# When the job of the token sums is spawned: ahead of attention's output product instead of behind it

## The chip, the cores and the metric

The kernel runs on one core of a Trainium2 chip. The metric is the device time of one execution in microseconds (us), as the median of several runs. The engines of the core are named as the profile names them: PE is the matrix engine (PEld its weight loads), DVE the vector engine, ACT the scalar engine, POOL and SP the other two; SP here only issues transfers (DMA). Each engine takes its instructions in the order in which the program lists them.

## The reference

Two layers act on x of 256 tokens by 2048 columns. Layer 0 mixes tokens by forgetting attention, layer 1 by dilated attention; behind each stands an MLP with a hidden width of 8192. Everything is float32. What matters here, cut down:

```python
def sq_relu_mlp(h, w_up, w_down):
    a = jax.nn.relu(h @ w_up)
    return (a * a) @ w_down

for i in range(DEPTH):
    h = rms_norm(x, mix_norm_g[i])
    mix = fox_attention(h, ...) if i % 2 == 0 else dilated_attention(h, ...)
    x = x + mix                       # the last step of attention is o @ w_out
    h = rms_norm(x, mlp_norm_g[i])
    x = x + sq_relu_mlp(h, mlp_w_up[i], mlp_w_down[i])
```

## The kernel before, in words

**Products.** A float32 product is made of three matmuls: each operand is split into a rounded high half and the low rest, and high x high, high x low and low x high are added in PSUM. The tokens are the stationary side (two blocks of 128), the weights the moving side (512 columns at a time). Weights arrive in *pieces* of 256 rows by 512 columns, in tiles `raw`, five of which exist. For each piece ACT writes the high half `wh` (L398, a cast), then DVE writes the low half `wl` (L399, a subtraction): together *the split* of the piece. Five tiles of each half exist too. A piece is 12 matmuls in an ordinary product (L447 to L449), 6 in a *slot* (below; L1114 to L1116). SP issues the loads of `raw` (L373); a tile is loaded again when its split is through.

**The program's order is made by ticks.** `product_steps` issues the matmuls of one step of 128 rows and then calls `jobs.tick()`; so an ordinary piece is two ticks and a slot one. When a piece's matmuls are issued, the split of the piece five further on is issued, just ahead of the tick that ends it. All other work is written as generators, *jobs*. A job yields a number (sleep so many ticks) or a key (sleep until another job has entered the key in `done`). `Jobs._run` goes once through the list of living jobs, oldest spawn first, and lets each that is due issue its instructions; it is called at each tick and at each spawn from outside. A key that a younger job enters is therefore seen by an older one at the next call only. `pin` fixes the order in which the instructions were issued, engine by engine. `clear(steps)` adds one tick where needed to end on a chosen parity of the tick count; slots flip that parity through `shift`.

**Around the change.** `out_proj` (attention's output product) makes four chunks of 512 columns of x: the first three interleaved (`group=3`), the fourth by itself, eight pieces. Behind each chunk `add_chain` adds it to x on DVE (L975) and spawns `norm_chain`, which sleeps 2 ticks, transposes the chunk on DVE and writes it to DRAM by SP (L531, L354), 3 ticks later has SP read it back, and after 11 more ticks (9 for the first chunk) splits it into `hT` (ACT L549, DVE L550), the stationary side of the MLP, two keys `(tag, pr)` a chunk, one tick apart. There are eight keys, `pr` 0 to 7. Later ACT takes sums of squares (`junk_n`, L614).

**The MLP** (`mlp`) opens with two chunks interleaved (pieces 0 to 15, counted from the MLP's start), the first 12 steps of the one, 12 of the other, and then the last 4 of each. Among the ordinary pieces that follow stand *slots*: some chunks of the up product are done with 7 products in place of 8 (Strassen-Winograd on 2x2 blocks), from sums of weight blocks (`sd`, `v`: L395, L401, L402 on DVE, ahead of or between the splits that use them) and from sums of token blocks. Up chunks that are through go by `up_chain` and `turn_up`: ACT takes relu and square (L1009, L1013, two each), DVE transposes (L1032), a round trip through DRAM follows, then ACT and DVE split again (L1057; L1061 and L1064).

**`token_sums(tag)`** makes the sums of token blocks, for both MLPs ("n1", "n3"), one *set* for each of the eight keys: four adds on DVE into one tile `room` (L563, L566, L567, L568), two ticks later a cast on ACT (L582), one tick later a subtraction on DVE (L586) that gives the low half; the last set has two of either. Each set first waits for its key and for `clear(4)` ticks. The first use of a set is a slot behind piece 15 (`jobs.need(("sums", tag, pr))`). The job issues no transfers. In the kernel before it is spawned by `mlp`, at L1143, when `out_proj` has issued everything.

Of the kernel before, what the change touches and what calls it, by code (L numbers as in the profile page):

```python
# [9 lines left out]
F32 = mybir.dt.float32  # L10
# [7 lines left out]
P = 128  # L18
# [101 lines left out]
def trunk(ctx: ExitStack, tc, x, fox_w_in, fox_b_f, fox_q_gain, fox_k_gain, fox_w_out, dil_w_in,  # L120
          dil_q_gain, dil_k_gain, dil_w_out, mix_norm_g, mlp_norm_g, mlp_w_up, mlp_w_down, out):
    nc = tc.nc
    jobs = Jobs()
# [4 lines left out]
    def clear(steps):  # L128

        return steps + (jobs.now + steps + 1 + shift[0]) % 2  # L130
# [21 lines left out]
    work = ctx.enter_context(tc.tile_pool(name="work", bufs=1))  # L152
# [317 lines left out]
    def in_group(new, steps, posts, parts=PARTS):  # L470


        banks = []
        for a, b in parts:
            for n, post in enumerate(posts):
                if a == 0:
                    banks.append(new(n))
                steps(banks[n], range(a, b))
                if b == KC:
                    jobs.spawn(post(banks[n]))  # L480
# [74 lines left out]
    def token_sums(tag):  # L555


        to = work.tile([P, 4, P], F32, tag="vw", name=f"room_{tag}", bufs=1)
        for pr in range(KC // 2):
            yield (tag, pr)  # L560
            yield clear(4)
            whole = hT[tag][pr]
            nc.vector.tensor_add(to.rearrange("p (i t) n -> p i (t n)", i=2), whole[:, :, 0, :].bitcast(F32),  # L563
                                 whole[:, :, 1, :].bitcast(F32))
            a12, a22, a11, a21 = (to[:, i, :] for i in range(4))
            nc.vector.tensor_add(a21, a21, a22)  # L566
            nc.vector.tensor_sub(a11, a11, a21)  # L567
            nc.vector.tensor_add(to[:, 0:2, :], to[:, 0:2, :], a11.unsqueeze(1).to_broadcast([P, 2, P]))  # L568
            yield 2
            if pr < KC // 2 - 1:  # L570
                split_sums = [[work.tile([P, 4, P], F32R, tag=SUM_TAGS[2 * pr + x], name=f"sums_{tag}_{pr}_{x}", bufs=1)
                               for x in range(2)]]
            else:
                three = [work.tile([P, 3, P], F32R, tag="s", name=f"sums_{tag}_{pr}_{x}", bufs=S_BUFS) for x in range(3)]
                split_sums = [three[0:2], (three[2][:, 0:1, :], three[2][:, 1:2, :])]
            sumT[tag, pr] = tuple([x[:, i, :] for x, _ in parts for i in range(x.shape[1])] for parts in
                                  (split_sums, [pieces[::-1] for pieces in split_sums]))
            at = 0
            spans = []
            for hi, lo in split_sums:  # L580
                spans.append(to[:, at:at + hi.shape[1], :])
                nc.scalar.copy(hi, spans[-1])  # L582
                at += hi.shape[1]
            yield 1
            for (hi, lo), of in zip(split_sums, spans):
                nc.vector.tensor_sub(lo, of, hi.bitcast(F32))  # L586
            jobs.done.add(("sums", tag, pr))
# [166 lines left out]
    def heads_pairs(name, slot):  # L754


        whole = work.tile([P, 2, 2, P], F32, tag=f"qkw{slot}", name=f"{name}w", bufs=1)
        q = work.tile([P, 2, 2, P], F32R, tag=f"q{slot}", name=f"{name}q", bufs=1)
        k = [work.tile([P, 2, S], F32R, tag=f"k{x}{slot + 3}", name=f"{name}k{x}", bufs=1) for x in "hl"]
        return (whole[:, 0], q[:, 0], q[:, 1]), (whole[:, 1], *k)  # L760

    def values(name):
        whole = work.tile([P, NC], F32, tag="vw", name=f"{name}w", bufs=1)
        both = work.tile([P, 2, NC], F32R, tag="v", name=f"{name}hl", bufs=1)
        return whole, both[:, 0], both[:, 1]
# [171 lines left out]
    def dilated(tag):  # L937
        for q4 in range(4):
            qTs, kTs = zip(*(heads_pairs(f"d{q4}_{g}", g) for g in range(3)))
            vt = values(f"dv{q4}")  # L940

            def heads_post(g):
                return lambda acc: qk_chain(acc, tag, ("dqk", q4, g),
                                            [(0, 2, DIL_G + g, qTs[g]), (2 * P, 2, DIL_G + 3 + g, kTs[g])])

            def value_post(acc):
                return v_chain(acc, tag, ("dv", q4), vt)

            if q4 == 0:
                in_group(lambda n: sums(), lambda acc, ks: product_steps(acc, keys_h(tag), lhs_h(tag), ks),  # L950
                         [value_post, heads_post(0)])
            for g in range(1 if q4 == 0 else 0, 3):
                product(keys_h(tag), lhs_h(tag), heads_post(g))
            for i in range(2):
                jobs.spawn(dil_head(q4, i, qTs, kTs, vt))
            if q4:
                product(keys_h(tag), lhs_h(tag), value_post)
# [33 lines left out]
    def out_proj(keys, lhs, then=None, ready=None, scale=None, group=0, parts=OUT_PARTS, late=False):  # L991
        posts = [lambda acc, n=n: add_chain(acc, n, then, ready, scale, late) for n in range(NX)]
        if group:
            in_group(lambda n: sums(*(() if n < 2 else (ps_sc, "sc") if scale else (ps_tp, "tp"))),
                     lambda acc, ks: product_steps(acc, keys(0), lhs, ks), posts[0:group], parts)
        for n in range(group, NX):
            if ready is not None and n == NX - 1:
                last_product(keys(n), lhs, final_add(n, scale))
            else:
                product(keys(n), lhs, posts[n])  # L1000
# [122 lines left out]
    def mlp(tag, **after):  # L1123
        aTs = [{} for b in range(4)]
        banks = []

        def one(b, n, what, pr):
            if pr == 0 and what in (0, 2):
                pools = ((ps_acc, f"acc{1 - turn['only']}"),) if what else ((ps_tp, "tp"), (ps_sc, "sc"))
                banks[2 * what:] = [pool.tile([P, NC], F32, tag=of, name=f"wide_{tag}_{b}_{n}_{of}{i}")  # L1130
                                    for pool, of in pools for i in range(2)]
            if what < 3:
                jobs.need(("sums", tag, pr))

            def then():
                if what == 2 and pr == KC // 2 - 1:
                    jobs.spawn(wide_chain(list(banks), tag, b, n, aTs[b]))
                if what == 3 and pr == KC // 2 - 2:
                    jobs.reach((f"{tag}a{b}", "crossed", n))

            slot_steps(tag, banks, what, pr, then)

        jobs.spawn(token_sums(tag))  # L1143
        woven.update(count=0, do=one, due={})
        for at, slot in wide_slots():
            woven["due"].setdefault(at, []).append(slot)
        for b in range(4):
            key = f"{tag}a{b}"
            aT = aTs[b]
            posts = [lambda acc, n=n, key=key, aT=aT: up_chain(acc, key, n, aT) for n in range(4)]  # L1150
            if b == 0:
                only = turn["next"]
                in_group(lambda n: sums(), lambda acc, ks: product_steps(acc, keys_h(tag), lhs_h(tag), ks), posts[0:2])
                turn["only"] = only
            for n in UP_ALONE[b]:
                product(keys_h(tag), lhs_h(tag), posts[n])

            def chunks(n):
                def at(k):
                    if n == NX - 1:  # L1160

                        jobs.done.add((tag, "free", b, k // 4 - 1))
                    return key, k // 4
                return at

            if b == 3:
                turn.update(next=turn["only"], only=None)
            out_proj(chunks,
                     lambda k: (aT[k // 4][0][:, k % 4, :], aT[k // 4][1][:, k % 4, :]),
                     scale=tag, group=3 if b == 3 else 0, parts=LAST_DOWN_PARTS, **(after if b == 3 else {"late": True}))  # L1170
            jobs.done.add((tag, "free", b, NX - 1))
        woven["do"] = None
# [66 lines left out]
    tag = "n0"  # L1239
    for j in range(4):  # L1240
# [10 lines left out]
        for hh in range(4):  # L1251
            jobs.spawn(fox_head(j, hh, qT, kT, vt))
        product(keys_h(tag), lhs_h(tag), lambda acc: v_chain(acc, tag, ("fv", j), vt))

    out_proj(lambda n: lambda k: ("of", k),
             lambda k: (oT["f", k // 4][0][:, k % 4, :], oT["f", k // 4][1][:, k % 4, :]),
             normed("n1", MLP_G), group=3)
    jobs.spawn(dilation_tables())
    mlp("n1", then=normed("n2", KC))
    dilated("n2")  # L1260
    out_proj(lambda n: lambda k: ("od", k // 2),
             lambda k: (oT["d", k // 4][0][:, k % 4, :], oT["d", k // 4][1][:, k % 4, :]),
             normed("n3", MLP_G + KC), group=3)
# [32 lines left out]
```

## Time and profile before

| what | value |
|---|---|
| median of 3 runs | 2091.22 us (2090.2 to 2091.6) |
| time of the profiled execution | 2090.77 us |
| its span from the first instruction to the last | 2089.0 us |
| PE, PEld busy | 2078.6 us, 1817.7 us |
| DVE, ACT, POOL busy | 1730.0 us, 1294.6 us, 275.2 us |
| granted clock of PE | 1.000 |

The page gives shares over the whole span; the stretches that matter lie at the two MLP beginnings, at 365 us ("n1") and at 1443 us ("n3"). A timeline row has the start, the time (for several instructions merged: from the first start to the last end), the engine, the line, out<-in, a count, and in brackets how long the engine was idle before and for whom. The time from one row's start to the next is what an instruction costs in a busy queue; it is a little shorter than its own duration, since neighbours overlap. A windows row has for a stretch each engine's busy time, then the granted clock and the transfers.

### The profile page before, as it was taken

The page shows a single profiled execution, that of the slowest core. Times are in us where ns is not written, and L with a number is a line of the kernel's source. Part 1 is how long each engine was busy: PE and PEld are TensorE (multiplying, and loading weights), DVE is VectorE, ACT ScalarE, POOL GpSimd, SP SyncE. Part 2 cuts the span into 40 slices and gives each one's busy share as a digit, 9 for nine tenths or more (in the row PEclk, how much of TensorE's full clock was granted, in tenths as well). Part 3 has the DMA queues.
Part 4 walks back from the last instruction along what each step waited for, and adds up shares of the span by engine and source line. Part 5 has one row for each costly group of instructions (what it writes and reads, how often), then busy time and mean ns, then how long its engine had stood idle before and what let it go on. Part 6 is the DMA issues. An engine that isn't in the chain of part 4 may idle for free.

```text
span 2089.0 us, 28961 instructions
## 1 busy us (share of the span) xinstructions
PE 2078.6 (100%) x9835; PEld 1817.7 (87%) x9835; DVE 1730.0 (83%) x2215; ACT 1294.6 (62%) x1777; POOL 275.2 (13%) x398
## 2 busy tenths in 40 slices
PE   9999999999999999999999999999999999999999
PEld 7888888878888888888888888888888888888888
DVE  6888876998989889888668787767998898899874
ACT  6665654766666667564656565655666666666662
POOL 2000000111212112120010010000113031212120
PEclk9999999999999999999999999999999999999999
DMA  8888887888888899897877876867879888899885
GB/s 258 255 262 261 257 248 215 272 262 265 269 282 268 264 296 274 262 289 246 278 242 230 248 241 210 268 205 235 269 247 277 281 276 263 276 280 281 263 282 164
DMA packets 357205, 539.04 MB, mean 258 GB/s; under 512 B 43752, under 2 KB 144448, under 8 KB 357056
## 3 DMA queue, kind: packets, MB, share of 16 engines
q1 hardware_dynamic: 334624, 507.41, 76.5%
q0 software_dynamic: 22016, 29.38, 6.2%
q8 instruction: 77, 1.26, 0.2%
q10 hardware_dynamic: 416, 0.39, 0.1%
q14 instruction: 72, 0.59, 0.1%
HBM read 484.09 MB, written 40.39 MB: 251 GB/s over the span
## 4 chain that ended last, share of the span: by engine, by line
PE 89%; DVE 6%; DMA 2%; ACT 1%; issue 1%; SPq 0%; POOL 0%; DVEq 0%; ACTq 0%; POOLq 0%
PE acc L448 23%; PE acc L447 23%; PE acc L449 23%; DVE wl L399 3%; PE wide_n_tp L1115 2%; PE wide_n_tp L1116 2%; PE wide_n_tp L1114 2%; PE wide_n_acc L1116 2%; PE wide_n_acc L1115 2%; PE wide_n_acc L1114 2%; PE wide_n_sc L1115 2%; PE wide_n_sc L1116 1%; PE wide_n_sc L1114 1%; DMA raw<-in_mlp_w_up_dram 1%; ACT wh L398 1%
## 5 line engine op out<-in xcount | busy, mean ns | idle before, releaser
L399 DVE TENSOR_TENSOR wl<-raw,wh 128x1024 fp32r<-128x1024 f32 (+1 forms) x763 | 918.6, 1213 | 303.3 <-ACT wh L398 293.8
L398 ACT CAST wh<-raw 128x1024 fp32r<-128x1024 f32 (+1 forms) x763 | 787.0, 1045 | 503.1 <-PE acc L449 360.8
L448 PE MATMUL acc<-wl,hT_n 128*128 128x512 f32 x1280 | 486.2, 380 | 4.0 <-DVE wl L399 3.8
L447 PE MATMUL acc<-wh,hT_n 128*128 128x512 f32 x1280 | 486.4, 380 | 0.1
L449 PE MATMUL acc<-wh,hT_n 128*128 128x512 f32 x1280 | 485.3, 379 | 0.0
L448 PEld LDWEIGHTS acc<-wl,hT_n 128*128 128x128 f32 x1280 | 242.1, 189 | 40.0 <-DVE wl L399 7.6
L449 PEld LDWEIGHTS acc<-wh,hT_n 128*128 128x128 f32 x1280 | 241.9, 189 | 34.4 <-DVE hT_n L606 0.4
L447 PEld LDWEIGHTS acc<-wh,hT_n 128*128 128x128 f32 x1280 | 242.1, 189 | 33.4 <-ACT hT_n L605 0.7
L447 PE MATMUL acc<-wh,aTh_n1a 128*128 128x512 f32 x512 | 194.0, 379 | 0.0
L448 PE MATMUL acc<-wl,aTh_n1a 128*128 128x512 f32 x512 | 194.0, 379 | 0.0
L449 PE MATMUL acc<-wh,aTl_n1a 128*128 128x512 f32 x512 | 194.0, 379 | 0.0
L447 PE MATMUL acc<-wh,aTh_n3a 128*128 128x512 f32 x480 | 181.9, 379 | 0.0
L448 PE MATMUL acc<-wl,aTh_n3a 128*128 128x512 f32 x480 | 181.9, 379 | 0.0
L449 PE MATMUL acc<-wh,aTl_n3a 128*128 128x512 f32 x480 | 181.9, 379 | 0.0
L970 POOL DMA_DIRECT2D x<-y_n x96 | 84.5, 1326 | 479.2 <-ACT y_n L969 421.0
L398 ACT CAST wh<-sd 128x1024 fp32r<-128x1024 f32 x80 | 84.1, 1051 | 98.1 <-DVE sd L395 75.8
L398 ACT CAST wh<-v 128x1024 fp32r<-128x1024 f32 x80 | 84.1, 1051 | 51.6 <-PE acc L449 41.5
L449 PEld LDWEIGHTS acc<-wh,aTl_n1a 128*128 128x128 f32 x512 | 96.8, 189 | 13.8
L447 PEld LDWEIGHTS acc<-wh,aTh_n1a 128*128 128x128 f32 x512 | 96.8, 189 | 13.7
L448 PEld LDWEIGHTS acc<-wl,aTh_n1a 128*128 128x128 f32 x512 | 96.8, 189 | 13.7
L399 DVE TENSOR_TENSOR wl<-v,wh 128x1024 fp32r<-128x1024 f32 x80 | 97.4, 1217 | 5.7 <-ACT wh L398 4.6
L449 PEld LDWEIGHTS acc<-wh,aTl_n3a 128*128 128x128 f32 x480 | 90.7, 189 | 12.9
(661 smaller groups left out, 3224.1 us busy)
## 6 DMA issues: line engine op xcount, KB each, us to landing
raw<-in_mlp_w_up_dram SPq DMA_DIRECT2D x296, 512.0 KB, 4.9
raw<-in_mlp_w_down_dram SPq DMA_DIRECT2D x256, 512.0 KB, 5.2
raw<-in_dil_w_in_dram SPq DMA_DIRECT2D x192, 256.0 KB, 3.7
raw<-in_fox_w_in_dram SPq DMA_DIRECT2D x94, 512.0 KB, 4.9
raw<-in_fox_w_out_dram SPq DMA_DIRECT2D x32, 512.0 KB, 4.9
raw<-in_dil_w_in_dram SPq DMA_DIRECT2D x32, 512.0 KB, 5.4
raw<-in_dil_w_out_dram SPq DMA_DIRECT2D x32, 512.0 KB, 4.5
x<-y_n POOLq DMA_DIRECT2D x96, 128.0 KB, 6.2
```

The lines of the kernel that those rows point to most:

```text
L398: nc.scalar.copy(hi[:, part, :], raw[:, part, :])
L399: nc.vector.tensor_sub(lo[:, part, :], raw[:, part, :], hi[:, part, :].bitcast(F32))
L447: nc.tensor.matmul(acc[t], ah[:, tok], hi, start=first, stop=False)
L448: nc.tensor.matmul(acc[t], ah[:, tok], lo, start=False, stop=False)
L449: nc.tensor.matmul(acc[t], al[:, tok], hi, start=False, stop=last)
L970: nc.gpsimd.dma_start(xt[n][:, t, h * HC:h * HC + HC], y, accum_op=ALU.add)
L1114: nc.tensor.matmul(banks[bank], ah, wh, start=what < 3 and of == 0, stop=False, **alone)
L1115: nc.tensor.matmul(banks[bank], ah, wl, start=False, stop=False, **alone)
L1116: nc.tensor.matmul(banks[bank], al, wh, start=False, stop=of == KC // 2 - 1, **alone)
```

## The change

The spawn of `token_sums` moves out of `mlp` to the place in `trunk` ahead of `out_proj`, for both MLPs. The generator then starts before its first key exists, so the tile `room` is allocated when the first key is there.

```diff
     def token_sums(tag):
 
 
-        to = work.tile([P, 4, P], F32, tag="vw", name=f"room_{tag}", bufs=1)
         for pr in range(KC // 2):
             yield (tag, pr)
+            if pr == 0:
+                to = work.tile([P, 4, P], F32, tag="vw", name=f"room_{tag}", bufs=1)
             yield clear(4)
...
-        jobs.spawn(token_sums(tag))
         woven.update(count=0, do=one, due={})
...
+    jobs.spawn(token_sums("n1"))
     out_proj(lambda n: lambda k: ("of", k),
...
     jobs.spawn(dilation_tables())
     mlp("n1", then=normed("n2", KC))
     dilated("n2")
+    jobs.spawn(token_sums("n3"))
     out_proj(lambda n: lambda k: ("od", k // 2),
```

## The prediction

> **What bounds the kernel now.** I read the page, then PE's waits, then the windows of the two MLP beginnings, then the timelines of DVE, ACT and SP there.
>
> ```profile
> span 2089.0 us, 28961 instructions
> PE 2078.6 (100%) x9835; PEld 1817.7 (87%) x9835; DVE 1730.0 (83%) x2215; ACT 1294.6 (62%) x1777; POOL 275.2 (13%) x398
> ```
>
> PE bounds it: matmuls follow one another without a gap.
>
> ```profile
> 365.03 0.38 PE L449 MATMUL acc<-wh,oTfl 128*128 128x512 f32 x1
> 365.25 0.38 PE L447 MATMUL acc<-wh,hT_n 128*128 128x512 f32 x1
> ...
> 456.22 0.48 PE L448 MATMUL acc<-wl,hT_n 128*128 128x512 f32 x1 [1.29 <-DVE wl L399]
> ```
>
> One matmul is 0.216 us, so a piece of 12 is 2.59 us, and "n1" starts at 365.25. Nothing gives PE less to do. A time can change only by PE waiting more or less, so I look for its waits.
>
> ```profile
> core 0: us, PE busy (x) PEld busy (x) DVE busy (x) ACT busy (x) POOL busy (x), PEclk, DMA share, GB/s
> 365.25:406.69 41.44, 41.44 (x194) 36.29 (x192) 37.27 (x69) 32.57 (x64) 1.07 (x1) 1.00 0.86 284
> 406.69:460.00 53.31, 50.82 (x230) 42.58 (x229) 51.45 (x70) 32.60 (x43) 13.20 (x24) 1.00 0.79 251
> 1484.80:1538.10 53.30, 50.87 (x230) 42.66 (x229) 51.44 (x70) 32.63 (x43) 13.05 (x24) 1.00 0.79 253
> ```
>
> From 406.69 to 460.00 run pieces 16 to 40: 13 ordinary pieces and 12 slots, 228 matmuls, 49.25 us at 0.216. They take 53.31, so PE loses 4.06 us, the last and largest loss at piece 39 (the row at 456.22, waiting for `wl`); "n3" loses the same. DVE is busy for 51.45 of the 53.31: here the splits are late because DVE has too much in front of them. These 8.1 us are all that could be won. The price of the sums, in DVE's and ACT's queues:
>
> ```profile
> 374.47 1.13 DVE L550 SCALAR_TENSOR_TENSOR hT_n<-turned_n,gain,hT_n 128x128 fp32r<-128x128 f32 x4
> 375.52 1.22 DVE L399 TENSOR_TENSOR wl<-raw,wh 128x1024 fp32r<-128x1024 f32 x1
> ...
> 377.70 1.30 DVE L531 STREAM_TRANSPOSE turned_n<-x 128x512 f32<-128x512 f32 x2
> 378.93 1.18 DVE L399 TENSOR_TENSOR wl<-raw,wh 128x1024 fp32r<-128x1024 f32 x1
> 380.03 0.68 DVE L563 TENSOR_TENSOR room_n<-hT_n 128x512 f32<-128x512 f32 x1
> ...
> 381.40 0.43 DVE L568 TENSOR_TENSOR room_n<-room_n 128x256 f32<-128x256 f32 x1
> 381.74 1.22 DVE L399 TENSOR_TENSOR wl<-raw,wh 128x1024 fp32r<-128x1024 f32 x1
> 383.46 1.23 DVE L399 TENSOR_TENSOR wl<-raw,wh 128x1024 fp32r<-128x1024 f32 x1 [0.50 <-ACT wh L398]
> 384.60 0.69 DVE L586 TENSOR_TENSOR sums_n<-room_n,sums_n 128x512 fp32r<-128x512 f32 x1
> 385.21 2.35 DVE L399 TENSOR_TENSOR wl<-raw,wh 128x1024 fp32r<-128x1024 f32 x2
> ...
> 391.30 1.22 DVE L399 TENSOR_TENSOR wl<-raw,wh 128x1024 fp32r<-128x1024 f32 x1 [0.89 <-ACT wh L398]
> ...
> 444.18 1.23 DVE L399 TENSOR_TENSOR wl<-raw,wh 128x1024 fp32r<-128x1024 f32 x1 [0.49 <-ACT wh L398]
> ...
> 446.17 1.23 DVE L399 TENSOR_TENSOR wl<-raw,wh 128x1024 fp32r<-128x1024 f32 x1 [0.16 <-ACT wh L398]
> ...
> 457.90 0.75 DVE L586 TENSOR_TENSOR sums_n<-room_n,sums_n 128x384 fp32r<-128x384 f32 x2
> 458.57 1.22 DVE L399 TENSOR_TENSOR wl<-raw,wh 128x1024 fp32r<-128x1024 f32 x1
> ```
>
> Four adds 1.71 us (380.03 to 381.74), a subtraction 0.60 (384.60 to 385.21; the last set's two 0.67, to 458.57), a split 1.14 on DVE.
>
> ```profile
> 381.86 0.62 ACT L582 CAST sums_n<-room_n 128x512 fp32r<-128x512 f32 x1 [1.73 <-DVE room_n L568]
> 382.38 2.94 ACT L398 CAST wh<-raw 128x1024 fp32r<-128x1024 f32 x3
> 386.25 1.04 ACT L398 CAST wh<-raw 128x1024 fp32r<-128x1024 f32 x1 [0.92 <-DMA raw<-in_mlp_w_up_dram]
> ...
> 390.22 1.05 ACT L398 CAST wh<-raw 128x1024 fp32r<-128x1024 f32 x1 [0.30 <-DMA raw<-in_mlp_w_up_dram]
> ...
> 403.80 1.08 ACT L1009 ACTIVATE a_n1a<-acc 128x512 f32<-128x512 f32 x2
> 404.77 1.15 ACT L1013 ACTIVATE a_n1a<-a_n1a 128x512 f32<-128x512 f32 x2
> 405.81 1.04 ACT L398 CAST wh<-raw 128x1024 fp32r<-128x1024 f32 x1
> ...
> 422.97 0.61 ACT L1057 CAST aTh_n1a<-back_n1a 128x512 fp32r<-128x512 f32 x1
> 423.49 1.04 ACT L398 CAST wh<-raw 128x1024 fp32r<-128x1024 f32 x1
> ```
>
> Every set makes ACT wait for the adds with its next high halves queued behind (the cast's row at 381.86), and DVE then for ACT (383.46): the queues stop one another.
>
> **The change part by part.** *How far it moves.* Count ticks from the end of `out_proj`'s first chunk; the MLP starts at tick 20. The first key is entered at tick 15. Before, the job is spawned at 20, adds 5 for parity: adds at tick 25, between the splits of pieces 6 and 7 (378.93 and 381.74). Now the job is older than the norm chains, sees the key at tick 16, and adds at 21. Each set takes about 8 ticks, so all eight move up by four ticks, two pieces: adds stood ahead of the splits of pieces 7, 11, 15, 19, 24, 29, 34, 39 and go ahead of 5, 9, 13, 17, 22, 27, 32, 37; the subtractions stood behind 8, 12, 16, 20, 25, 30, 35, 40 and go behind 6, 10, 14, 18, 23, 28, 33, 38. Allocating `room` later costs nothing: its last owner, attention's values, is done. No transfer, and no wait of a slot for a set, is touched: the first set is there at 385 and the first slot is at 406.69.
>
> *At once.* The first adds now stand ahead of the `hT` split at 374.47 and of pieces 5 and 6. Piece 6 is due on PE at 365.25 + 6 x 2.59 = 380.8, its low half 0.22 later; its `wl` ends at 378.93 + 1.18 = 380.1, now 1.71 later, 381.8: PE loses 0.8 there. That isn't added to the later losses, since a PE that is late by 0.8 has 0.8 more to wait for later splits; only the largest lateness counts, and that is piece 39's.
>
> *At piece 39, DVE's own order:* its adds stood ahead of it already; the last subtractions come ahead of it too, +0.67. Against it: the second set's subtraction (0.60) falls into the 0.89 that DVE idles at 391.30, -0.60.
>
> *New waits of DVE for ACT.* Each time, the cast starts when the adds end, the high half of a later piece stands behind it, and DVE has little to do meanwhile. From the adds' end, with 0.07 for two hand-overs: piece 18: cast 0.52 + `wh` 1.04 = 1.63, DVE has one split, 1.05 left, wait 0.58. Piece 19: ACT goes on with relu and square, 1.56 + 0.97 + 1.04 + 1.04 = 4.60, DVE has 3.38, wait 1.22. Piece 23: 0.52 + 1.04 (squares) + 1.04 + 0.07 = 2.67 against a split and `sd`, 2.19: 0.50. Piece 28: 0.52 + 0.52 (L1057) + 1.04 + 0.07 = 2.15 against 1.05: 1.10. Sum +3.40. The waits at 444.18 and 446.17, which come from a cast standing just there, go: 0.49 + 0.16 and what the overlap gave, -0.60 (I take the smaller, rounded). So each MLP: 0.67 - 0.60 + 3.40 - 0.60 = +2.87.
>
> *A transfer that comes later.*
>
> ```profile
> 378.44 3.72 SPq L354 DMA_DIRECT2D blocks_n<-turned_n  x8
> 382.26 0.39 SPq L373 DMA_DIRECT2D raw<-in_mlp_w_up_dram  x1
> 382.76 1.14 SPq L354 DMA_DIRECT2D turned_n<-blocks_n  x2
> 383.95 1.15 SPq L373 DMA_DIRECT2D raw<-in_mlp_w_up_dram  x2
> ```
>
> The transposes at 377.70 slip by 1.71, so do SP's eight writes, and the load of piece 12 queued behind them (383.95); ACT's `wh` for it at 390.22 waits for that load already. Between 0 (the transfer lands as early as before) and 1.71; in "n1" I take 1.7, since the issue itself is that late. In "n3" the old spawn also ran the job list once; without it the last norm chain starts a tick later, and its read-back goes behind this load instead of ahead of it: I take 0.5.
>
> Sum: 2.87 + 1.7 + 2.87 + 0.5 = +7.9. On the profiled execution, 2090.77 + 7.9 = 2098.7; the median shown is 0.45 above that execution: 2099.1.
>
> Two rules of the Trainium skill pull apart here. "TensorE: Matmul & The Clock Gate", section "Architectural detail", says that ACT and DVE are strict first-in first-out; the waits at 381.86 and 383.46 agree, and by it the sum stands at +7.9. "Perfetto Trace Analysis", section "Optimization Strategy", says to find the gaps of the bounding engine and make what they wait for start sooner; that would make the time go the other way, and is the third rival.
>
> **The rivals.** *No difference to speak of:* DVE and ACT absorb the new waits, as the idle 0.89 absorbs one subtraction, and the load lands as before. Then 0.67 - 0.60 an MLP is left, 2091.4; with half of the net 2.80 of waits it is 2.8 more, 2094.2. For it: ACT is busy for only 32.6 of 53.3 us. Against it: it is idle because it is queued behind the adds.
>
> *Worse:* the late load repeats. Loads wait for `wl`, and a late `wl` sends them late, so that each MLP pays 1.7 once more and "n3" the full 1.7: 2099.1 + 3.4 + 1.2 = 2103.7. Against it: between 406.69 and 460.00 the transfers take 0.79 of their time.
>
> *Faster:* sums made sooner take work out of the stretch in which PE loses. The place is DVE's queue ahead of piece 39, the price the 8.1 us of losses: 2091.2 - 8.1 = 2083.1 at best. It decides once DVE has over 2 us an MLP less in front of piece 39; I find 0.60, and 0.60 of ACT's waits. The skill's rule of starting sooner is this case.
>
> **How the numbers follow.** My forecast 0.65, no difference 0.22, worse 0.08, faster 0.05. About 0.2%, 4.2 us, is what a measurement of this kernel can tell from no change: slower than 2095.4 is the forecast with the worse case, 0.73; within it 0.22; faster than 2087.0 0.05. The range runs from 2092.5 (most of the rival's span is in) to 2103.7.
>
> **What would show it.** In the profile after: adds ahead of the `hT` split of the third chunk; a PE loss of about 0.8 us near 381 in "n1"; DVE waits for `wh` of 0.5 to 1.2 us at pieces 18, 19, 23 and 28, which lie near 407, 409, 419 and 430, and none at 444; PE losses up to piece 39 of some 4.06 + 4.6 = 8.6 us in "n1" (the 0.8 among them) and 4.06 + 3.4 = 7.4 in "n3", with large steps at pieces 24 and 32 already, ahead of which a set of adds now stands. I am wrong if DVE's queue reaches piece 39 no later than now, or if the last loss isn't there; and wrong in the load if `wh` of piece 12 starts before 391.

## The result, and the profile after

The changed kernel takes 2101.41 us (median of 6 runs, 2100.55 to 2104.26) against 2090.96 us of the kernel before on the same chips (6 runs): a ratio of 1.0054, with a 95% interval of 1.0041 to 1.0067. It is slower by 10.45 us, where +7.9 was forecast. The profiled execution took 2100.55 us. From L562 to L1142 its lines stand one higher than before (L569 is the old L568, L583 the cast, L587 the subtraction, L1010 the relu).

The page, and the windows of the same pieces as before (0 to 15, then 16 to 40, of "n1", then of "n3"):

```profile
span 2098.8 us, 28964 instructions
PE 2083.3 (99%) x9835; PEld 1821.2 (87%) x9835; DVE 1730.9 (82%) x2215; ACT 1294.5 (62%) x1777; POOL 276.3 (13%) x398
```

```profile
core 0: us, PE busy (x) PEld busy (x) DVE busy (x) ACT busy (x) POOL busy (x), PEclk, DMA share, GB/s
366.53:409.03 42.50, 41.97 (x193) 36.13 (x192) 36.45 (x69) 28.85 (x58) 1.61 (x1) 1.00 0.80 267
409.03:466.72 57.69, 52.58 (x229) 43.54 (x228) 53.93 (x71) 36.24 (x48) 13.19 (x24) 0.97 0.75 239
...
1491.61:1547.91 56.30, 52.06 (x229) 43.88 (x228) 52.73 (x67) 34.94 (x46) 13.06 (x24) 0.97 0.77 236
```

The same instructions, the same DVE time. Pieces 16 to 40 need 49.25 us at 0.216 a matmul; they took 53.31 before and take 57.69 in "n1" and 56.30 in "n3", and the first 16 pieces of "n1" lose 1.0 as well. That is +5.4 us in "n1" and +3.0 in "n3". A sum over the whole trace agrees: adding, for every two neighbouring matmuls between 60 and 2000 us, what their starts are apart beyond 0.216, gives 8.66 us before and 17.35 after. (The bracket of a PE row counts from the modelled end of the matmul before and shows about 0.16 us less than such a difference.) The granted clock of 0.97 in those two windows is new. Another 1.3 us are lost ahead of the first MLP, which starts at 366.53 in place of 365.25: the opening's matmuls are still 0.43 us apart at 9 us, where before they are 0.22 apart from 6.5 us on. The profiles of the kernels below show that in some and not in others, whether or not the jobs start early (MLP start at 365.25 with "n1" early alone, at 366.58 with the sets at the old place and 8 ticks apart), so nothing here puts it down to the change.

DVE's timeline has the order that was forecast, and its new waits:

```profile
374.65 1.27 DVE L976 TENSOR_TENSOR x<-x,acc 128x512 f32<-128x512 f32 x2
375.84 0.68 DVE L564 TENSOR_TENSOR room_n<-hT_n 128x512 f32<-128x512 f32 x1
...
377.55 1.13 DVE L550 SCALAR_TENSOR_TENSOR hT_n<-turned_n,gain,hT_n 128x128 fp32r<-128x128 f32 x4
378.60 1.22 DVE L399 TENSOR_TENSOR wl<-raw,wh 128x1024 fp32r<-128x1024 f32 x1
...
394.48 1.22 DVE L399 TENSOR_TENSOR wl<-raw,wh 128x1024 fp32r<-128x1024 f32 x1 [2.11 <-ACT wh L398]
...
411.50 1.23 DVE L399 TENSOR_TENSOR wl<-raw,wh 128x1024 fp32r<-128x1024 f32 x1 [0.50 <-ACT wh L398]
414.45 1.23 DVE L399 TENSOR_TENSOR wl<-raw,wh 128x1024 fp32r<-128x1024 f32 x1 [1.13 <-ACT wh L398]
423.53 1.23 DVE L399 TENSOR_TENSOR wl<-raw,wh 128x1024 fp32r<-128x1024 f32 x1 [0.41 <-ACT wh L398]
435.14 1.23 DVE L399 TENSOR_TENSOR wl<-raw,wh 128x1024 fp32r<-128x1024 f32 x1 [1.02 <-ACT wh L398]
```

The adds (375.84) stand ahead of the third chunk's `hT` split (377.55). The row at 394.48 is piece 12, whose load came late; ACT's timeline says so:

```profile
393.40 1.04 ACT L398 CAST wh<-raw 128x1024 fp32r<-128x1024 f32 x1 [2.76 <-DMA raw<-in_mlp_w_up_dram]
```

The last four are pieces 18, 19, 23 and 28. What PE waited for in the end stands in its own timeline, the two long waits of "n1" and what follows the first of them:

```profile
377.95 0.48 PE L449 MATMUL acc<-wh,hT_n 128*128 128x512 f32 x1 [0.46 <-DVE hT_n L550]
...
428.47 0.48 PE L1116 MATMUL wide_n_sc<-wl,sums_n 128*128 128x512 f32 x1 [2.10 <-DVE wl L399]
428.79 0.38 PE L1117 MATMUL wide_n_sc<-wh,sums_n 128*128 128x512 f32 x1
429.00 0.38 PE L1115 MATMUL wide_n_sc<-wh,sums_n 128*128 128x512 f32 x1
...
430.01 0.63 PE L447 MATMUL acc<-wh,hT_n 128*128 128x512 f32 x1
430.43 0.63 PE L448 MATMUL acc<-wl,hT_n 128*128 128x512 f32 x1
...
432.85 0.38 PE L448 MATMUL acc<-wl,hT_n 128*128 128x512 f32 x1
...
447.90 0.48 PE L447 MATMUL acc<-wh,hT_n 128*128 128x512 f32 x1 [2.16 <-ACT a_n1a L1010]
```

Two things here were not in the forecast. At 447.90, the start of piece 32, PE waits for ACT's relu (L1010): the next up chunk uses the PSUM bank that the relu still has to read, and the relu stands in ACT's queue behind the cast of the seventh set, which waits for DVE's adds:

```profile
445.79 0.62 ACT L583 CAST sums_n<-room_n 128x512 fp32r<-128x512 f32 x1 [2.20 <-DVE room_n L569]
446.31 1.04 ACT L398 CAST wh<-v 128x1024 fp32r<-128x1024 f32 x1
447.26 1.08 ACT L1010 ACTIVATE a_n1a<-acc 128x512 f32<-128x512 f32 x2
```

And behind the wait at 428.47 matmuls start 0.43 us apart in place of 0.216 from 429.22 to 432.6: PE runs at half clock for 3.4 us and loses 1.7. "n3" shows the same behind its wait of 2.5 us for the relu. Of the 8.7 us that PE loses more than before, 3.4 are so spent at half clock; that doesn't mean that the time would be 3.4 us shorter without it, as the part on the prediction shows.

### The profile page after: what moved, and what is told of

It is laid out like the page before. It is cut to its first block, busy times and chain, and to the rows that moved or that the text cites. A ratio compares the mean times of both kernels' runs of the same rounds, so it can differ in the third digit from the quotient of the medians.

```text
span 2098.8 us, 28964 instructions
## 1 busy us (share of the span) xinstructions
PE 2083.3 (99%) x9835; PEld 1821.2 (87%) x9835; DVE 1730.9 (82%) x2215; ACT 1294.5 (62%) x1777; POOL 276.3 (13%) x398
## 4 chain that ended last, share of the span: by engine, by line
PE 85%; issue 7%; DVE 5%; ACT 1%; DMA 1%; POOL 0%; SPq 0%; ACTq 0%; DVEq 0%; POOLq 0%
PE acc L447 22%; PE acc L448 22%; PE acc L449 22%; PE wide_n_tp L1116 2%; PE wide_n_tp L1117 2%; PE wide_n_tp L1115 2%; DVE wl L399 2%; PE wide_n_acc L1116 2%; PE wide_n_acc L1115 2%; PE wide_n_acc L1117 2%; PE wide_n_sc L1116 2%; PE wide_n_sc L1115 2%; PE wide_n_sc L1117 2%; ACT wh L398 1%; DMA raw<-in_mlp_w_up_dram 0%
## 5 line engine op out<-in xcount | busy, mean ns | idle before, releaser
L971 POOL DMA_DIRECT2D x<-y_n x96 | 84.5, 1322 | 480.6 <-ACT y_n L970 421.9
L448 PEld LDWEIGHTS acc<-wl,aTh_n3a 128*128 128x128 f32 x480 | 90.7, 189 | 12.9
```

Of the source, the lines that this page charges most:

```text
L448: nc.tensor.matmul(acc[t], ah[:, tok], lo, start=False, stop=False)
L971: nc.gpsimd.dma_start(xt[n][:, t, h * HC:h * HC + HC], y, accum_op=ALU.add)
```

## The experiments

**One MLP at a time.** The early spawn for "n1" alone, then for "n3" alone; the other MLP's job is spawned in `mlp` as before.

```diff
-    jobs.spawn(token_sums("n3"))
...
+        if tag == "n3":
+            jobs.spawn(token_sums(tag))
         woven.update(count=0, do=one, due={})
```

> The early spawn for the first MLP (n1) alone. Theory of the two queues (DVE waits for ACT behind early casts, PE then for wl and for the relu that empties a bank): the whole +5.4 us of PE waits that n1 showed, among them 1.5 us at half clock behind a wait of over 2 us, so +5.4 us on before; n3 shows its old 4.0 us of waits. Rival (the start of the kernel, or something common to both, costs it): half of the +10.4 us or less in n1's own window, the rest elsewhere.

> The early spawn for the second MLP (n3) alone. Theory of the two queues: +3.1 us on before, of which 1.5 us at half clock; n1 shows its old 4.1 us of waits. Rival (only the late load of piece 12 costs, and n3 has none): no difference from before.

2095.83 us, ratio 1.0025 (1.0014 to 1.0037), and 2094.83 us, 1.0022 (1.0013 to 1.0031); before took 2090.18 beside them. +5.65 and +4.65, each with an interval of some 2 us either way, add up to 10.3: the two MLPs are the whole of it, and nothing common to both shows. In the profiles PE's losses grow by 6.0 us in "n1" in the first run (from 4.1 to 10.1, the half clock now behind the wait for the relu) and by 2.7 in "n3" in the second (from 4.0 to 6.7). In the first run "n3", whose order is that of before, loses 3.1 in place of 4.0: 1 us can come and go without a change of order.

**The sets put back.** Early spawns, but the first set sleeps 8 ticks.

```diff
-            yield clear(4)
+            yield clear(4 if pr else 8)
```

> Both spawns early, but the first set sleeps 8 ticks in place of 4, so that all sets stand where they stood before; only the last norm chain of n3 stays one tick later. Theory (only the place of the sets in the queues counts): the time of before within 0.1%, PE waits of 4.1 us in n1 at the old places. Rival (the place in the job list or the tile's later allocation costs): the time of after, +10 us, or a good part of it.

2090.53 us, ratio 1.0002 (0.9993 to 1.0012). Only the place of the sets in the queues counts. The one thing left different is n3's last norm chain, a tick later; "n3" loses 3.2 us in place of 4.0, but it lost as little in the run above that left its order alone, so the chain is not shown to be the reason.

**The cast on another engine, at both places.**

```diff
-                nc.scalar.copy(hi, spans[-1])
+                nc.gpsimd.tensor_copy(hi, spans[-1])
```

> As after, with the cast of the sums made by POOL in place of ACT; DVE's order is unchanged. Theory (of the +10 us most is ACT's queue held by a cast that waits for DVE's adds): DVE's waits of 0.5, 1.1, 0.4 and 1.0 us at pieces 18, 19, 23 and 28 go, PE's waits from piece 16 on fall from 8 to about 5 us in n1 and from 5.6 to about 3 in n3, so 5 to 9 us faster than after (POOL's cast costs nobody unless it takes over 3 us, or slows DVE beside it). Rival (DVE's adds standing earlier are the cost by themselves): within 3 us of after.

> As before (sums at their old place), with the cast made by POOL. Theory: the two waits of DVE for ACT at 444 and 446 us go (0.65 us), so 0.5 to 2 us faster than before; and after with POOL casts against this one is the price of the early adds alone, which the theory puts at 0 to 2 us. Rival: the early adds alone cost 7 us or more, so this one is that much faster than the early spawn with POOL casts.

With the early spawn 2096.84 us, ratio 1.0032 (1.0022 to 1.0043); at the old place 2092.65, 1.0010 (1.0000 to 1.0019). Both expectations missed: the early spawn became some 4 us faster than after, between the theory's 5 to 9 and the rival's 3, and the old place became slower. The early spawn costs 10.45 us with casts on ACT and 4.2 with casts on POOL, neither the 0 to 2 of the theory nor the 7 or more of the rival. DVE's waits between 407 and 470 us, in the early kernel with POOL's casts:

```profile
DVE wl L399 <- ACT wh L398: 0.6, 1, 0.6
```

and with ACT's, in the changed kernel:

```profile
DVE wl L399 <- ACT wh L398: 3.0, 4, 1.1
```

(total, times, longest). The four waits are gone, and with them, by the times, six tenths of the cost; by PE's losses in the profiles (9.3 us at the old place, 14.1 early) a little over four tenths of the 8.7. What stays is the wait of 2.17 us at piece 12, and 2.5 us at piece 32, now for `wl`.

The edit takes away more than the waits' cause, though, for it makes DVE slower. Two splits that run while POOL casts take 2.77 us, where two took 2.35 (in the kernel before, at 385.21):

```profile
430.03 2.77 DVE L399 TENSOR_TENSOR wl<-raw,wh 128x1024 fp32r<-128x1024 f32 x2
...
430.17 1.54 POOL L583 CAST sums_n<-room_n 128x512 fp32r<-128x512 f32 x1 [1.11 <-DVE room_n L569]
```

Every split of over 1.3 us up to piece 39 overlaps a cast on POOL, in both runs, and none is as long where ACT casts. From the first MLP's start to the end of piece 39's split DVE is busy for 88.3 us with POOL's casts, and for 85.5 with ACT's in the run with "n1" early alone; at the old place for 86.0 and, with the sets put back, 84.5. So the two runs show that the casts on ACT carry part of the cost, and not how large a part.

**One cast alone.** As after, with the seventh set's cast and subtraction three ticks later, behind the relu; the shorter sleep of the eighth set keeps its adds where they were.

```diff
-            yield clear(4)
+            yield 2 if pr == 7 else clear(4)
...
-            yield 2
+            yield 5 if pr == 6 else 2
```

> As after, but the cast and the subtraction of the seventh set stand three ticks later, behind the relu of the third up chunk; the adds stay where they are. Theory (PE's wait of 2.2 to 2.5 us at piece 32 comes from that cast, which holds ACT's queue with the relu behind it): that wait goes, and in n3 the half clock behind it; 0 to 1 us of later wl lateness comes back, so 2 to 4 us an MLP, 4 to 7 us faster than after. Rival (DVE's earlier adds are the cost and ACT would be late anyway): the wait at piece 32 stays over 1.5 us or comes back at piece 39, within 1.5 us of after.

2098.59 us, ratio 1.0039 (1.0025 to 1.0053): 8.4 us over the before beside it, 2.0 less than after, between the two theories. The wait for the relu goes, but at the same piece 32 PE then waits for `wl`, behind that set's adds:

```profile
446.48 0.48 PE L448 MATMUL acc<-wl,hT_n 128*128 128x512 f32 x1 [1.49 <-DVE wl L399]
```

In "n3" that wait is 1.89 us, and half clock follows as in the changed kernel. So the relu was the last of two things to end there, by some 0.6 us; the other is DVE's order. PE's losses fall from 9.5 to 8.4 us in "n1" and from 7.1 to 6.4 in "n3", and 1.0 of this lies in the first 16 pieces of "n1", which the edit doesn't touch.

**The load of piece 12.** First "n3" made like "n1" (one run of the job list ahead of its MLP), then "n1" like "n3" (its last norm chain one tick later).

```diff
+    jobs._run()
     mlp("n3", ready=store)
```

```diff
-             normed("n1", MLP_G), group=3)
+             normed("n1", MLP_G, lambda n: 3 if n == 3 else 2), group=3)
```

> As after, with one run of the job list ahead of the second MLP, so that n3's last norm chain starts at the tick it started at before, as in n1. Theory (n3 was cheaper than n1 by 2.4 us because its read-back went one tick later and the load of piece 12 ahead of it): n3 then shows what n1 shows, DVE waits 2 us for piece 12, PE waits rise from 7.1 to about 9.5 us, and the time by 1.5 to 2.5 us on after. Rival (the two MLPs differ by the phase of the clock gate alone): no difference.

> As after, with n1's last norm chain one tick later, so that the read-back of its transposes is issued behind the load of piece 12, as in n3. Theory (n1's DVE wait of 2.1 us at piece 12 comes from that load being queued behind the read-back): the wait falls to under 0.5 us and n1's PE waits from 9.5 to 6 to 8 us, so 1 to 3 us faster than after. Rival (the load is late because DVE's splits release the tiles late, whatever SP's order): the wait stays over 1.5 us and the time within 1 us of after.

2102.43 us, ratio 1.0055 (1.0040 to 1.0070), and 2098.63, 1.0037 (1.0023 to 1.0050). In the first a wait of 1.44 us for piece 12 appears in "n3", as long as before the change (1.43), and PE's losses there go from 7.1 to 8.2, less than expected; the time's +1.0 is within the spread. In the second DVE's wait in "n1" falls from 2.11 to 0.69:

```profile
392.64 1.23 DVE L399 TENSOR_TENSOR wl<-raw,wh 128x1024 fp32r<-128x1024 f32 x1 [0.69 <-ACT wh L398]
```

PE's losses fall from 9.5 to 7.2, and the time is 8.1 us over the before beside it, 2.3 less than after. The load was late because SP issued the read-back first. The tick is worth the 1.4 us by which DVE's wait falls; 1.0 of PE's 2.4 us lies in the first 16 pieces again, which lose as little in the run of one cast alone.

**Other spacings of the sets.** The ticks ahead of each set, 4 before; the old place, once the early one:

```diff
-            yield clear(4)
+            yield clear(8)
```

> As before, with 8 ticks in place of 4 ahead of each set: sets every 12 ticks, the last at tick 109 in place of 81; the slots need them at ticks 53 to 121. Theory (the 4.1 us of waits an MLP come from DVE having five sets of 2.3 us in front of it between 407 and 460 us): about two sets move behind 460, where DVE is busy 73.7 of 80 us, and the waits fall to 0 to 2 us an MLP, 4 to 7 us faster than before. Rival (the losses come from the slots' own sd and v work): within 1 us of before.

> The early spawn with 8 ticks ahead of each set in place of 4: sets every 12 ticks from tick 21. Theory (what costs is how many sets stand between 407 and 460 us and which splits they meet, not the early start): most of the +10 us goes, 0 to 3 us faster than before, near the 2088.4 of the same spread from the old place. Rival (the early start itself costs): at least 4 us slower than the same spread from the old place.

> The old place with 6 ticks ahead of each set: sets every 10 ticks, the last at tick 95. Between before (8 ticks apart, 8.7 us of PE waits between 60 and 2000 us) and 12 ticks apart (4.2 us, now behind 490 us). Theory (DVE's load between 407 and 460 us sets the waits, and sets that go behind 460 meet the next dense stretch): 3 to 6 us of waits, 2 to 6 us faster than before. Rival (any other phase of the sets against the splits loses as the early spawn did): slower than before.

> The old place, 4 ticks ahead of each of the first three sets and 8 ahead of the other five: adds at ticks 25, 33, 41, 53, 65, 77, 89 and 101. Between 12 ticks apart throughout (last set at 109, 4.2 us of PE waits, all behind 490 us) and 8 apart (8.7 us, all before 540). Theory (the load of DVE counts, summed up to each split): the three quick sets use idle time of DVE and the last set is out of the way before 490, so 2 to 5 us of waits, 2083 to 2090 us. Rival (the phase of the late sets against splits and slots decides, as at 10 ticks apart): 6 us of waits or more, 2091 us or slower.

| ticks ahead of a set | place | time, us | ratio to before | PE loss, 60 to 2000 us |
|---|---|---|---|---|
| 8 | old | 2088.41 | 0.9990 (0.9981 to 0.9999) | 4.15 us |
| 8 | early | 2090.35 | 0.9999 (0.9990 to 1.0008) | 6.22 us |
| 6 | old | 2094.93 | 1.0020 (1.0012 to 1.0029) | 11.50 us |
| 4 for three sets, then 8 | old | 2085.45 | 0.9978 (0.9968 to 0.9987) | 2.84 us |

With 8 ticks the early spawn costs 2 us where it cost 10 with 4, so the early start as such is not the price. The spread by 8 gained less than expected: hardly a wait is left up to piece 40, but new ones of up to 1 us come behind 490, for the split of the up chunks (L1064) and for `wl`. And 6 ticks, a smaller step in the good direction, is slower than before: there the rival held, and the load of DVE alone doesn't tell the time. That it is which splits and casts each set meets is the rival's account; for 6 ticks it was not taken apart. The last row is faster than both kernels. Its windows:

```profile
406.69:460.00 53.31, 53.31 (x247) 46.40 (x247) 52.03 (x65) 34.26 (x43) 13.24 (x24) 1.00 0.85 270
460.00:540.00 80.00, 79.11 (x364) 68.14 (x363) 74.73 (x84) 54.36 (x70) 20.21 (x32) 1.00 0.85 265
```

PE is busy for all of the 53.31 us in which it lost 4 before, while DVE is busy for 52.03 of them, against 51.45 before: DVE can be full and late for nobody, if what stands in front of each split is short enough.

## Why the prediction came out right, by its own steps

- **How far the sets move:** as forecast: the adds and subtractions of all eight sets stand ahead of and behind the splits that it names, in both MLPs.
- **At once:** 0.8 us at piece 6 of "n1" was forecast; 0.7 us for `hT` (377.95) and 0.3 at piece 6 came. The price of the adds also fell on `hT`, which stands between them and the split; the step named it and didn't price it. As forecast, this is not added to what comes later.
- **New waits of DVE for ACT:** 0.58, 1.22, 0.50 and 1.10 us forecast, 0.50, 1.13, 0.41 and 1.02 measured; the two at 444 and 446 are gone. That is net 2.4 us an MLP where 2.8 were forecast, and the largest term of the path. A term that was missing: in both MLPs DVE now also waits 0.59 us for POOL (`rstd_n`, L626), as it did not before.
- **The late load:** +1.7 us taken for "n1"; `wh` of piece 12 started 24.97 us behind the MLP's start before and 26.87 after, +1.9. DVE's wait there grew by 1.2 (0.89 to 2.11), where the sum has 1.7 less 0.6. For "n3" 0.5 was taken, and there the term has the wrong sign: DVE waited 1.43 us for piece 12 before and doesn't wait now. The reason given, the read-back's place on SP, held in the runs that moved it.
- **Only piece 39's lateness counts:** this held in "n1" and failed in "n3". The split of piece 39 and the matmul that takes it up, before (PE's row at 456.22 stands in the prediction) and after:

```profile
454.95 1.22 DVE L399 TENSOR_TENSOR wl<-raw,wh 128x1024 fp32r<-128x1024 f32 x1
```

```profile
461.68 1.22 DVE L399 TENSOR_TENSOR wl<-raw,wh 128x1024 fp32r<-128x1024 f32 x1
...
462.95 0.48 PE L448 MATMUL acc<-wl,hT_n 128*128 128x512 f32 x1 [0.24 <-DVE wl L399]
```

In "n1" this split ends 90.9 us behind the MLP's start before and 96.4 after, and PE takes it up at once both times. On the way to it no row of DVE waits for PE. So all of the +5.4 us is DVE's lateness at piece 39, where 4.6 were forecast; the longer waits at pieces 24 and 32 and the half clock are the same lateness, met earlier. In "n3" the split ends only 2.0 us later than before (90.9 to 92.8 us behind the start), where 3.4 were forecast, and PE comes to it 1.25 us late: the last loss isn't there, which the prediction had named as a sign of being wrong. What is late there is PE itself, behind the wait for the relu, which the prediction left out, and the half clock behind that. In the profiles half clock followed the wait for the relu in six MLPs, and in each PE comes to this split 1.25 us late; in the two where it didn't follow, PE waits for the split and takes it up within 0.06. So in these profiles the wait for the relu alone costs nothing by piece 39, and half clock behind it costs 1.2 us.
- **The sum:** 4.6 and 3.4 us were forecast, and PE loses 5.4 and 3.1 more by its trace. That "n3" came so close is luck: 2.0 us of DVE's path and 1.2 of a clock that the prediction doesn't know. What the median has beyond these 8.5 us is not explained by the change's path; in the profiled execution it is the 1.3 us of the opening.
- **The rivals:** no difference failed because DVE did not absorb the waits in a stretch where it was busy for 51.45 of 53.31 us. Worse lies as far from the measured time as the forecast does, 2.3 us, but failed in its mechanism: up to piece 40 only the load of piece 12 held DVE longer than before, and only in "n1". Faster, starting sooner what PE waits for, failed because PE never waited for the sums; it waited for splits in the same queues, which the sooner sums pushed back.

## What to carry to other kernels

Work that nobody is waiting for should not be issued earlier just because its inputs are there: in a queue that is nearly full it delays what stands behind it. A step that goes from one engine to another and back (add, cast, subtract) needs other work between its parts on both engines, or each queue stops the other; count what stands between them, instruction by instruction. Waits of the bounding engine are not added up: find the last one, and ask what its releaser's own queue was late by. Before moving such a step, list for every engine what is queued behind its waiting part, also the reads that free a PSUM bank.

## What was not expected of the hardware

PE's clock fell to half behind short waits. Measured from one matmul's start to the next beyond 0.216, the profiles here have 17 waits of 2.05 to 2.62 us. Behind 11 of them, 0.4 to 1.3 us after the wait's end, matmuls start 0.43 us apart for 3.41 us (1.7 us lost); behind none of those of 1.0 to 1.65 us do they. The same wait of 2.26 us at piece 24 of "n1" led to it in three profiles and not in two.

What decides can be read from the traces. The two slow stretches of the changed kernel begin at 429.28 and 1528.37, which is 1099.09 us apart, or 322 times 3.4133. The first of them, with the stretches of the same length around it (the last number but two is the granted clock):

```profile
425.87:429.28 3.41, 1.31 (x7) 0.83 (x6) 3.41 (x6) 1.99 (x2) 1.68 (x4) 1.00 0.88 276
429.28:432.70 3.42, 3.42 (x10) 2.61 (x9) 3.32 (x6) 0.00 (x0) 2.65 (x5) 0.50 0.87 273
432.70:436.11 3.41, 3.41 (x18) 2.98 (x17) 2.39 (x3) 3.09 (x5) 0.00 (x0) 1.00 0.69 252
```

Lay such a grid of 3.413 us over each profile, through its own changes of clock. Each of the 11 waits then has 2.05 us or more within one interval, and the next interval is the slow one. The 6 others are cut by a line of the grid and have at most 1.80 us on either side; the one at 447.90 is cut at 446.35 into 0.76 and 1.56. So in these profiles the idle time within one interval decides, with the limit between 1.80 and 2.05 us, and where the lines fall differs from execution to execution.

The Trainium skill ("TensorE: Matmul & The Clock Gate", section "What's actually happening") describes a window of 3.4 us that runs freely and halves the clock after one idle window. The length of the slow stretch and the grid agree; that the idle time has to fill a window does not, since 2.05 us were enough.
